# A hybrid attention block on one core: the value loops' banks in two pools, the first key pair's loads inside the value loops, the opening's sums in other banks

## The chip, the core and the metric

The kernel runs on one core of a Trainium2 chip. Five engines with queues of their own work side by side: TensorE (PE, matrix products; the loading of its stationary operand is listed apart as PEld), VectorE (DVE), ScalarE (ACT), GpSimd (POOL) and SyncE (SP), which here only issues transfers. SP and POOL issue the transfers; POOL issues those that add to what is in the destination, and those that depend on its own work. The metric is the device time of one execution in microseconds (us). PE writes into PSUM, eight banks of 512 floats per partition; all other tiles lie in SBUF.

## The reference, cut to what matters

One decoder block on x of 512 tokens by 2048, all in float32: one input projection, two groups of heads, one output projection.

```python
h = _rmsnorm(x, norm_g)
qa, kca, vca, ksa, vsa, kwa, vwa, za, ga, qb, kb, vb, zb = jnp.split(h @ w_in, offsets, axis=-1)
# group A: 8 heads of 128, 2 key/value heads
kc = _compress(_rope(kca), cmp_k_pos, cmp_k_w1, cmp_k_w2)
vc = _compress(vca, cmp_v_pos, cmp_v_w1, cmp_v_w2)
o_cmp, p_cmp = _compressed_attention(qa, kc, vc)
o_sel = _selected_attention(qa, _rope(ksa), vsa, _select_blocks(p_cmp, S))
o_win = _banded_attention(qa, _rope(kwa), vwa, WIN_A)
gates = jax.nn.sigmoid(ga)
y_a = (gates[0] * o_cmp + gates[1] * o_sel + gates[2] * o_win) * jax.nn.silu(za)
# group B: 16 heads of 64, a window of 128 with sinks
y_b = _banded_attention(_rope(qb), _rope(kb), vb, WIN_B, sink=sinks) * jax.nn.silu(zb)
x = x + jnp.concatenate([y_a, y_b], axis=-1) @ w_out
return _rmsnorm(x, final_g)
```

`_compress` takes overlapping blocks of 32 tokens, adds a position table, and sends each block of 32 x 128 numbers through a small two-layer network (w1, silu, w2).

## The kernel before

**Words.** Each float32 operand of a product is split into a high word (rounded, `whi`, `xh`) and a low word (the rest, `wlo`, `xl`), and a product is three matmuls: high by high, high by low, low by high (`mm3`, L107 to L110). So each weight tile is loaded (SP), copied to its high word (ACT, L88 or L517) and subtracted to its low word (DVE, L89 or L518) before PE can use it. There are three buffers for each of the two words, and four for loaded weights, `raw0` to `raw3`.

**Order.** The program is written as one Python function; a scheduler with a model of time orders the instructions of each engine when it is built. Each engine then works through its own queue in that order, and waits at an instruction until its operands and its buffer are free. A tile of a pool is a buffer; a new tile of the same name waits for the last reader of the old one. A pool that takes the room of a closed pool waits for that pool's readers.

**Stages around the change.**

1. Opening (to 60 us). The tokens are loaded, scaled and split; four projections run meanwhile into the six banks of pool `ps0`. Then two sums of squares over the tokens, `psr` and `psc` (L173 to L177), become `rstdb` and `rstd` by ACT (L178, L179) and DVE. `bank(6)` and `bank(7)` are tiles of `psp`, the pool of two banks called `pj` that all projections use.
2. Sliding-window heads (60 to 290). Eight steps of scores, softmax and `attn_b` (L362 on) while PE computes the projections of the next ones (`proj`, L207). `attn_b` ends with a read of its bank `opb` by ACT (L387) and DVE (L388).
3. Value loops (290 to 369, L764 to L780). `tok_chunk` multiplies token chunks into the value accumulators: four units of `wv1` into banks 4 and 5 of pool `ps1`, then eight of `wv0` into banks 0 to 3. Between them `compress_unit` (L646) adds one unit of the compression network to an accumulator `cacc`, each with two loads of `cw`. `build(6)` and `build(7)` make gate weights and sums of token rows (DVE, L408 to L414); the parts stored to `wd` are later loaded over `xh` and `xl` by POOL (L794). `v_evac` (L478) reads the value accumulators.
4. Key pairs `keys(1)` and `keys(0)` (369 to 430), then eight query and gate pairs, `pair(h)` (L634), one per head of group A, between the heads' attention, `attn_a`. Each pair of projections is computed by `seven` (L541): seven products over quarters of the weights instead of eight, called "22", "p", "21", "12", "w", "u" and "q" after what they add up. Products use quarters x1 to x4 and their sums; `tags` says which of `raw0` to `raw3` holds which. For a key pair (`extra`), a fifth buffer `raw5` takes a sum of two quarters, loaded plainly by SP and added to by an accumulating transfer of POOL, and a second such transfer adds into x4 (L565 to L568).
5. Behind the pairs the heads' attention ends and the output projection follows (690 to 843).

In a pair, `turn` applies the rotary table to the query and `q_split` splits it into `qh` and `ql`. For heads 0 to 6 the last add of `turn` and the subtraction for `ql` are on POOL, for head 7 on DVE.

Of the kernel before, what the change touches and what calls it, by code (L numbers as in the profile page):

```python
# [34 lines left out]
def hybrid_block(ctx, tc, xT, xtm, w0, wv0, wv1, wz, wq, wo0, wos, cw1, cw2, cpos, e2, rope, tabs, sinks, gT, fg, out):  # L35
# [134 lines left out]
            o = i * P  # L170
            mm3(acc0[i], hi[:, o:o + P], lo[:, o:o + P], xh[:, k, :], xl[:, k, :], k == 0, k == KT - 1)

    psr = bank(6)  # L173
    pe.matmul(psr, ones, sqa, start=True, stop=True)
    psc = bank(7)
    for t in range(NQ):
        pe.matmul(psc[:, t:t + 1], sqa[:, t * P:(t + 1) * P], ones[:, 0:1], start=True, stop=True)  # L177
    act.activation(rstdb, psr, AF.Sqrt, bias=eps, scale=1.0 / D)  # L178
# [317 lines left out]
            pool.dma_start(Vd[e, :, :, w], other[e].bitcast(F32))  # L496

    ps1s = ExitStack()
    ps1 = ps1s.enter_context(tc.tile_pool(name="ps1", bufs=1, space=PSUM, side="left"))

    def bank(i):
        return ps1.tile([P, S], F32, name=f"bank{i}", tag=f"bank{i}")

    cw2s = pp.tile([P, 2, 2, P], F32, name="cw2s")
    nc.sync.dma_start(cw2s, cw2)
# [22 lines left out]
            ah, al = xf[op, m]  # L528
            mm3(bank, u[0][:, cs], u[1][:, cs], ah, al, new and m == 0, m == 7, not new)

    tags = ["raw0", "raw1", "raw2", "raw3"]

    def load_quarter(src, tag, quarter):
        t = weights(tag)
# [7 lines left out]
    def seven(i, early=(), done=None, hooks=None, extra=None, final=False):  # L542
        src = wq[i]
        early = list(early)
        hooks = hooks or {}
        c1, c2, c4, c3 = tags
        tags[:] = c4, c1, c3, c2

        def load(tag, quarter):
            return early.pop(0) if early else load_quarter(src, tag, quarter)  # L550

        def plus(out, a, b, op=ALU.add):
            return dve.tensor_tensor(out=out, in0=a, in1=b, op=op).ins  # L553

        pa, pb = [psp.tile([P, S], F32, name="pj", tag="pj") for e in range(2)]
        qv = wk.tile([P, S], F32, name="t1", tag="t1", bufs=1)
        zr = wk.tile([P, S], F32, name="zr", tag="xr", bufs=1)
        d, jj = qv[:, H1], zr[:, H0]
        x1 = load(c1, 3)
        u0 = unit(x1)  # L560
        x2 = load(c2, 0)
        u3 = unit(x2)
        x4 = load(c4, 2)
        if extra:
            sm = extra()  # L565
            last["dma"] = nc.sync.dma_start(sm, src[0]).ins
            pool.dma_start(sm, src[2], accum_op=ALU.add)
            pool.dma_start(x4, src[3], accum_op=ALU.add)  # L568
        else:
            sm = x2  # L570
            with ExitStack() as behind:
                if "jj" in last:
                    behind.enter_context(tc.issue_after(last["jj"]))
                plus(x2, x2, x4)
        prod(pb[:, H0], u0, "22", True)
        act.activation(d, pb[:, H0], AF.Copy, scale=-1.0)
        if final:
            act.activation(zr[:, H1], pb[:, H0], AF.Copy)
        run(hooks, "22")
        x3 = load(c3, 1)  # L580
        prod(pa[:, H0], u3, "p", True)
        plus(d, d, pa[:, H0])
        run(hooks, "p")
        if not final:
            u2 = unit(x3)
            prod(pb[:, H0], u2, "21", False)
            act.activation(zr[:, H1], pb[:, H0], AF.Copy)
            plus(jj, d, zr[:, H1])
            run(hooks, "21")
        u4 = unit(sm)  # L590
        if not extra:
            plus(x4, x4, x1)
        plus(sm, sm, x1)
        prod(pa[:, H0], u4, "12", False)
        act.activation(qv[:, H0], pa[:, H0], AF.Copy)
        plus(jj, d if final else jj, qv[:, H0], ALU.subtract)
        run(hooks, "12")
        u1 = unit(x4)
        prod(pa[:, H1], u1, "w", True)
        plus(d, d, pa[:, H1])  # L600
        run(hooks, "w")
        u5 = unit(sm)
        plus(sm, sm, x3)
        prod(pb[:, H1], u5, "u", True)
        last["u"] = recent["mm"]
        plus(d, d, pb[:, H1])
        first = done(qv)
        run(hooks, "u")
        u6 = unit(sm)
        prod(pb[:, H1], u6, "q", False)  # L610
        last["jj"] = plus(jj, jj, pb[:, H1])
        run(hooks, "q")
        if final:
            with tc.issue_after(last["u"]):
                u2 = unit(x3)
                prod(pa[:, H0], u2, "21", True)
            plus(zr[:, H1], zr[:, H1], pa[:, H0])
            plus(jj, jj, zr[:, H1])
        return first, zr
# [13 lines left out]

    def pair(h, hooks=None):  # L634
        def q_done(qv):
            turn(qv, engine=pool if h < 7 else dve)
            return q_split(qv, pool if h < 7 else dve)

        qq, zr = seven(2 + h, done=q_done, hooks=hooks, final=h == 7)
        last["jj"] = dve.tensor_tensor(out=zr, in0=zr, in1=rstdb, op=ALU.mult).ins  # L640
        st = wk.tile([P, S], F32, name="st", tag="st")
        act.activation(st, zr, AF.Tanh, scale=0.5)
        dve.scalar_tensor_tensor(out=st, in0=st, scalar=1.0, in1=zr, op0=ALU.add, op1=ALU.mult)
        return qq, st
# [38 lines left out]
        return sl  # L683

    def compressed_keys(acc):
        sl = compress_hidden(acc, bank(4))
        kcp = bank(5)
        for i in range(2):
            pe.matmul(kcp[:, 0:64], cw2s[:, 0, i, :], sl[:, i, :], start=i == 0, stop=i == 1)
        kct = pp.tile([P, 64], F32, name="kct")  # L690
        act.activation(kct, kcp[:, 0:64], AF.Copy, scale=0.5)
        k1 = pp.tile([P, 2, CMP], F32R, name="k1w")
        for g, (h, l) in enumerate(((KH[:, 0:CMP], KL[:, 0:CMP]), (k1[:, 0], k1[:, 1]))):
            src = kct[:, g * 32:g * 32 + 32]
            act.activation(h, src, AF.Copy)
            dve.tensor_tensor(out=l, in0=src, in1=h.bitcast(F32), op=ALU.subtract)
        for e in range(2):
            pool.dma_start(Kd[e, :, 0:CMP], k1[:, e].bitcast(F32))

    def compressed_values(acc):  # L700
        sl = compress_hidden(acc, bank(4))
        for g in range(2):
            sr = wk.tile([P, 2, 4, 32], F32, name="sr", tag="pcr", bufs=1)
            for i in range(2):
                dve.tensor_copy(sr[:, i], sl[:, i, g * 32:g * 32 + 32].unsqueeze(1).to_broadcast([P, 4, 32]))
            vcp = bank(5 - g)
            for i in range(2):
                pe.matmul(vcp[:, 0:P], sr[:, i].rearrange("p a b -> p (a b)"), cw2s[:, 1, i, :], start=i == 0,
                          stop=i == 1)
# [17 lines left out]
                pool.dma_start(Kd[e, :, CMP:].rearrange("p (t w c) -> p w t c", w=2, c=P)[:, w],  # L727
                                  views[e].bitcast(F32))

    def fifth():  # L730
        return pp.tile([P, 1056], F32, name="raw5", tag="kvt0")[:, 0:1024]

    def keys(g, hooks, early=()):
        def one(v):
            turn(v)
            key_words(v, g, 0)

        zr = seven(1 - g, early, done=one, hooks=hooks, extra=fifth)[1]

        def other():  # L740
            turn(zr)
            key_words(zr, g, 1)

        return other
# [15 lines left out]
        turned(kc[g], kvts[0][:, g, :, 0:32])  # L760
    for g in range(2):
        values(proj(wz[18 + g]), g)
    cacc = [psp.tile([P, S], F32, name="pj", tag="pj") for e in range(2)]
    xr = rows(6)  # L764
    for u in range(4):
        tok_chunk(wv1, 4, 256, vacc[1], u, True)
# [6 lines left out]
            build(7, xr)  # L773
    for u in range(8):
        tok_chunk(wv0, 2, 280, vacc[0], u, False)
        compress_unit(1, u, cacc[1])
        if u == 0:
            v_evac(1, vacc[1])
        if u == 1:
            compressed_keys(compress_sum(cacc[0]))  # L780

    def gate_evac():
        for t in range(NQ):
# [3 lines left out]
        gc = gates[:, 0, :].rearrange("p (h b) -> p h b", b=3)[:, :, 0]  # L787
        dve.tensor_scalar(gc, gc, rowvalid, None, op0=ALU.mult)

    early = [load_quarter(wq[0], c, quarter) for c, quarter in zip(tags, (3, 0, 2, 1))]  # L790
    with tc.issue_after(last["lo"]):
        for ms in (slice(0, 4), slice(4, 8)):
            for e in range(2):
# [568 lines left out]
```

## Time and profile before

| | us |
|---|---|
| median of three runs | 844.12 |
| the three runs | 840.61, 844.12, 848.92 |
| the profiled execution | 845.09 |
| its span | 843.3 |
| PE busy | 807.7 (96%) |
| DVE busy | 688.8 (82%) |
| ACT busy | 500.4 (59%) |
| POOL busy | 97.4 (12%) |

The profile is of one execution, whose own time is 845.09 us; the span of 843.3 runs from its first to its last instruction. All positions are us from the span's start. A row of a timeline has the start, the duration, the engine, the line, the operation, and the tile written and the tiles read; in brackets is how long the engine had been idle before it and what ended that. "x2" means two such instructions in a row. A row of waits has who waited, for what, how long in total, how often, and the longest. Lines such as L108 are lines of the kernel before; a helper's line stands for all its callers, so the tile names tell the caller.

### The profile page before, as it was taken

To read this page: it belongs to the slowest core of one execution; us is meant where nothing else is said; L and a number is where in the kernel's file an instruction comes from. 1 tells how busy PE (TensorE), PEld (TensorE's weight loads), DVE (VectorE), ACT (ScalarE), POOL (GpSimd) and SP (SyncE) were. 2 spreads that over 40 slices of the span, in tenths; PEclk is the share of its full clock that TensorE was granted. 3 is DMA by queue.
4 is the path that set the end of the run, shared out by engine and by line. 5 is a ranking of instruction groups with operands and counts; after the bars stand their busy time and mean duration, and the time that the engine had idled before them with its cause. 6 is when DMAs were issued, how large, how long until landed. Compare 5 with 4: busy or idle time off the path is not lost.

```text
span 843.3 us, 15353 instructions
## 1 busy us (share of the span) xinstructions
PE 807.7 (96%) x5738; PEld 751.2 (89%) x5738; DVE 688.8 (82%) x1404; ACT 500.4 (59%) x1092; POOL 97.4 (12%) x93
## 2 busy tenths in 40 slices
PE   9989999999999899989899999999989899999996
PEld 7777888888888789989799999999989799999996
DVE  6768988988897567748889998998998978777995
ACT  6635655645555346654447678777677767544545
POOL 3514000000010001332101110110010000010000
PEclk9999999999999999999999999999999999999998
DMA  8552143144343338967333223234245126796845
GB/s 283 164 175 93 58 150 114 62 125 150 125 136 115 126 86 267 293 206 200 125 101 83 65 67 113 62 104 164 89 146 167 51 79 249 223 229 203 231 114 200
DMA packets 45450, 122.12 MB, mean 145 GB/s; under 512 B 5408, under 2 KB 7488, under 8 KB 45376
## 3 DMA queue, kind: packets, MB, share of 16 engines
q1 hardware_dynamic: 41504, 108.00, 39.2%
q0 software_dynamic: 3584, 12.62, 7.2%
q8 instruction: 45, 0.74, 0.4%
q10 hardware_dynamic: 288, 0.52, 0.2%
q14 instruction: 29, 0.24, 0.1%
HBM read 108.77 MB, written 12.35 MB: 144 GB/s over the span
## 4 chain that ended last, share of the span: by engine, by line
PE 72%; DVE 12%; DMA 6%; ACT 5%; issue 4%; SPq 0%; POOL 0%; DVEq 0%; ACTq 0%; POOLq 0%
PE pj L108 14%; PE pj L109 14%; PE pj L110 14%; PE oa L109 4%; PE oa L110 4%; PE oa L108 4%; PE sp L832 3%; DVE wlo L518 2%; PE bank L109 2%; DMA raw<-wq 2%; PE bank L108 2%; PE bank L110 2%; PE tp L371 1%; DVE raw L553 1%; DVE wlo L89 1%
## 5 line engine op out<-in xcount | busy, mean ns | idle before, releaser
L108 PE MATMUL pj<-xh,whi 128*128 128x256 f32 (+1 forms) x608 | 204.2, 336 | 8.6 <-ACT rstdb L178 2.7
L110 PE MATMUL pj<-xh,wlo 128*128 128x256 f32 (+1 forms) x608 | 203.0, 334 | 0.9 <-DVE wlo L518 0.8
L109 PE MATMUL pj<-xl,whi 128*128 128x256 f32 (+1 forms) x608 | 203.1, 334 | 0.0
L108 PEld LDWEIGHTS pj<-xh,whi 128*128 128x128 f32 x608 | 115.0, 189 | 20.8 <-ACT rstdb L178 2.8
L110 PEld LDWEIGHTS pj<-xh,wlo 128*128 128x128 f32 x608 | 114.8, 189 | 12.0 <-DVE wlo L518 1.5
L109 PEld LDWEIGHTS pj<-xl,whi 128*128 128x128 f32 x608 | 114.9, 189 | 11.1 <-issue 0.7
L89 DVE TENSOR_TENSOR wlo<-raw,whi 128x1024 fp32r<-128x1024 f32 (+2 forms) x72 | 80.9, 1127 | 31.1 <-ACT whi L88 26.5
L517 ACT ACTIVATE whi<-raw 128x1024 fp32r<-128x1024 f32 x70 | 73.3, 1056 | 49.2 <-PE pj L109 20.9
L88 ACT ACTIVATE whi<-raw 128x1024 fp32r<-128x1024 f32 (+2 forms) x71 | 65.0, 920 | 61.1 <-PE pj L109 48.1
L518 DVE TENSOR_TENSOR wlo<-raw,whi 128x1024 fp32r<-128x1024 f32 x70 | 87.0, 1252 | 12.1 <-ACT whi L517 11.8
L109 PE MATMUL oa<-wlo,yh 128*128 128x256 f32 x200 | 55.9, 280 | 0.2 <-DVE wlo L1185 0.2
L110 PE MATMUL oa<-whi,yl 128*128 128x256 f32 x200 | 55.8, 279 | 0.0
L108 PE MATMUL oa<-whi,yh 128*128 128x256 f32 x200 | 55.6, 279 | 0.0
L108 PE MATMUL pj<-pu,whi 128*128 128x256 f32 x160 | 45.6, 285 | 4.0 <-ACT a L672 1.8
L110 PE MATMUL pj<-pu,wlo 128*128 128x256 f32 x160 | 45.0, 281 | 0.0
L109 PE MATMUL pj<-pu,whi 128*128 128x256 f32 x160 | 44.7, 280 | 0.0
L272 DVE TENSOR_TENSOR pl<-tp,ph 128x512 fp32r<-128x512 f32 x56 | 37.6, 683 | 6.2 <-ACT ph L271 5.9
L350 ACT ACTIVATE ttb<-ttb,sums 128x256 f32<-128x256 f32 (+1 forms) x64 | 30.0, 471 | 16.7 <-DVE sums L343 16.5
L271 ACT ACTIVATE ph<-tp 128x512 fp32r<-128x512 f32 x56 | 31.7, 590 | 12.4 <-PE tp L867 11.1
L553 DVE TENSOR_TENSOR raw<-raw 128x1024 f32<-128x1024 f32 x32 | 38.9, 1216 | 0.1
L109 PEld LDWEIGHTS oa<-wlo,yh 128*128 128x128 f32 x200 | 37.8, 189 | 0.4 <-DVE wlo L1185 0.4
L110 PEld LDWEIGHTS oa<-whi,yl 128*128 128x128 f32 x200 | 37.8, 189 | 0.0
(372 smaller groups left out, 2340.3 us busy)
## 6 DMA issues: line engine op xcount, KB each, us to landing
raw<-wq SPq DMA_DIRECT2D x42, 512.0 KB, 4.1
raw<-wz SPq DMA_DIRECT2D x36, 512.0 KB, 3.9
cw<-cw SPq DMA_DIRECT2D x32, 256.0 KB, 4.2
raw<-wos SPq DMA_DIRECT2D x12, 512.0 KB, 6.5
rw<-wos SPq DMA_DIRECT2D x10, 512.0 KB, 5.4
xr<-xT SPq DMA_DIRECT2D x16, 256.0 KB, 4.4
rows<-xT SPq DMA_DIRECT2D x8, 512.0 KB, 5.2
raw<-wo SPq DMA_DIRECT2D x8, 512.0 KB, 3.8
```

What stands on the lines that cost most here:

```text
L88: last["hi"] = act.activation(hi[:, :width], rw[:, :width], AF.Copy).ins
L89: last["lo"] = dve.tensor_tensor(out=lo[:, :width], in0=rw[:, :width], in1=hi[:, :width].bitcast(F32), op=ALU.subtract).ins
L108: pe.matmul(ps, ah, bh, start=first, stop=False, skip_group_check=go_on)
L109: pe.matmul(ps, ah, bl, start=False, stop=False, skip_group_check=go_on)
L110: recent["mm"] = pe.matmul(ps, al, bh, start=False, stop=last, skip_group_check=go_on).ins
L271: act.activation(ph, tp, AF.Copy)
L272: dve.tensor_tensor(out=pl, in0=tp, in1=ph.bitcast(F32), op=ALU.subtract)
L350: act.activation(tv, tv, AF.Exp, bias=mn[:, e, v:v + 1], scale=-1.0, accum_out=dn[:, e, v:v + 1])
L517: act.activation(hi, src, AF.Copy)
L518: last["lo"] = dve.tensor_tensor(out=lo, in0=src, in1=hi.bitcast(F32), op=ALU.subtract).ins
L553: return dve.tensor_tensor(out=out, in0=a, in1=b, op=op).ins
L832: pe.matmul(sp[:, a:b], qq[:, qs], kk[:, ko:ko + b - a], start=pi == 0, stop=pi == 2)
```

## The change

**Opening.** The two sums of squares go to banks 0 and 1 of `ps0` instead of the two `pj` buffers.

**Value loops.** Pool `ps1` of six banks becomes two pools, banks 0 to 3 on the left and banks 4 and 5 on the right. The second compression accumulator is bank 4, taken when the first value loop's accumulators have been read out, and no longer a `pj` buffer; the small banks of the compressed keys and values are renumbered to fit. The accumulator of the compressed keys is copied one unit earlier.

**Key pairs.** `tags` starts with another order, so that x1 of the first pair lies in `raw3`. Inside the second value loop, x1 is loaded at unit 3, and the first pair's sum at unit 4; the other three quarters are loaded behind the loop. The second pair's sum gets a buffer of its own (`kvt1`). For a key pair `tags` is turned once more, so that the next pair finds other buffers.

**Query pairs.** Head 6 has its last rotary add and its `ql` on DVE, as head 7.

```diff
-    psr = bank(6)
+    psr = bank(0)
...
-    psc = bank(7)
+    psc = bank(1)
...
-    ps1 = ps1s.enter_context(tc.tile_pool(name="ps1", bufs=1, space=PSUM, side="left"))
+    ps1 = [ps1s.enter_context(tc.tile_pool(name=f"ps1{side[0]}", bufs=1, space=PSUM, side=side)) for side in ("left", "right")]
 
     def bank(i):
-        return ps1.tile([P, S], F32, name=f"bank{i}", tag=f"bank{i}")
+        return ps1[i // 4].tile([P, S], F32, name=f"bank{i}", tag=f"bank{i}")
...
-    tags = ["raw0", "raw1", "raw2", "raw3"]
+    tags = ["raw3", "raw0", "raw1", "raw2"]
...
         x4 = load(c4, 2)
         if extra:
             sm = extra()
-            last["dma"] = nc.sync.dma_start(sm, src[0]).ins
-            pool.dma_start(sm, src[2], accum_op=ALU.add)
             pool.dma_start(x4, src[3], accum_op=ALU.add)
+            tags[:] = c2, c1, c4, c3
...
-            turn(qv, engine=pool if h < 7 else dve)
-            return q_split(qv, pool if h < 7 else dve)
+            turn(qv, engine=pool if h < 6 else dve)
+            return q_split(qv, pool if h < 6 else dve)
...
-    def fifth():
-        return pp.tile([P, 1056], F32, name="raw5", tag="kvt0")[:, 0:1024]
+    def fifth(n):
+        return pp.tile([P, 1056], F32, name="raw5", tag=f"kvt{n}")[:, 0:1024]
+
+    def sums(t, src, first, other):
+        last["dma"] = nc.sync.dma_start(t, src[first]).ins
+        pool.dma_start(t, src[other], accum_op=ALU.add)
+
+    def fifth_sum(g):
+        if ready:
+            return ready.pop()
+        t = fifth(1)
+        sums(t, wq[1 - g], 0, 2)
+        return t
...
-        zr = seven(1 - g, early, done=one, hooks=hooks, extra=fifth)[1]
+        zr = seven(1 - g, early, done=one, hooks=hooks, extra=lambda: fifth_sum(g))[1]
...
-    cacc = [psp.tile([P, S], F32, name="pj", tag="pj") for e in range(2)]
+    cacc = [psp.tile([P, S], F32, name="pj", tag="pj"), None]
+    early, ready = [], []
...
         tok_chunk(wv0, 2, 280, vacc[0], u, False)
-        compress_unit(1, u, cacc[1])
         if u == 0:
             v_evac(1, vacc[1])
+            csum = compress_sum(cacc[0])
+            cacc[1] = bank(4)
+        compress_unit(1, u, cacc[1])
         if u == 1:
-            compressed_keys(compress_sum(cacc[0]))
+            compressed_keys(csum)
+        if u == 3:
+            early.append(load_quarter(wq[0], tags[0], 3))
+        if u == 4:
+            ready.append(fifth(0))
+            sums(*ready, wq[0], 0, 2)
...
-    early = [load_quarter(wq[0], c, quarter) for c, quarter in zip(tags, (3, 0, 2, 1))]
+    early += [load_quarter(wq[0], c, quarter) for c, quarter in zip(tags[1:], (0, 2, 1))]
```

**Where instructions moved.** On PE at the start of the value loops (banks 4 and 5 are the first value accumulators, `pj_2913` the last projection ahead of the compression), before:

```order
L110 MATMUL bank4_2837<-whi_2980,xl_105 128x256
L108 MATMUL bank5_2838<-whi_2980,xh_104 128x256
L108 MATMUL pj_2913<-xh_104,whi_2915 128x512
L109 MATMUL pj_2913<-xl_105,whi_2915 128x512
L110 MATMUL pj_2913<-xh_104,wlo_2916 128x512
```

and in the changed kernel, where that projection is `pj_2916`:

```order
L108 MATMUL bank5_2841<-whi_2982,xh_104 128x256
L109 MATMUL bank5_2841<-wlo_2983,xh_104 128x256
L110 MATMUL bank5_2841<-whi_2982,xl_105 128x256
L108 MATMUL pj_2916<-xh_104,whi_2918 128x512
L109 MATMUL pj_2916<-xl_105,whi_2918 128x512
```

Before, the projection came after 31 of the first value unit's 48 matmuls, and the other 17 followed it; now it comes after all 48.

On DVE in the same place (`cw` and `wlo_3066` belong to the compression, `rows` to `pu` to `build(6)`, `kvt1<-pj` is the read-out of that projection, `wlo_3102` the second value unit's low word), before:

```order
L747 TENSOR_TENSOR kvt1_2830<-pj_2913,rstdb_68 128x16x32
L518 TENSOR_TENSOR wlo_3066<-cw_3067,whi_3065 128x512
L518 TENSOR_TENSOR wlo_3066<-cw_3071,whi_3065 128x512
L408 TENSOR_TENSOR rows_2977<-rows_2977 128x256
L409 SCALAR_TENSOR_TENSOR rows_2977<-rows_2977,gt_70 128x256
L656 COPY F_3258<-posw_2826 128x4x2 x2
L410 SCALAR_TENSOR_TENSOR rows_2977<-rows_2977,gt_70 128x256
L89 TENSOR_TENSOR wlo_3102<-raw_3100,whi_3101 128x1024
L414 SCALAR_TENSOR_TENSOR qw1_600<-rows_2977,gt_70,qw0_599 128x256
```

and in the changed kernel, where that low word is `wlo_3104`:

```order
L518 TENSOR_TENSOR wlo_3068<-cw_3073,whi_3067 128x512
L408 TENSOR_TENSOR rows_2979<-rows_2979 128x256
L409 SCALAR_TENSOR_TENSOR rows_2979<-rows_2979,gt_70 128x256
L410 SCALAR_TENSOR_TENSOR rows_2979<-rows_2979,gt_70 128x256
L414 SCALAR_TENSOR_TENSOR qw1_600<-rows_2979,gt_70,qw0_599 128x256
L414 SCALAR_TENSOR_TENSOR pu3_594<-rows_2979,pu1_592 128x256
L411 TENSOR_TENSOR rows_2979<-rows_2979 128x256
L414 SCALAR_TENSOR_TENSOR pu7_598<-rows_2979,pu5_596 128x256
L414 SCALAR_TENSOR_TENSOR wf_3085<-rows_2979,wf_3085 128x256
L757 TENSOR_TENSOR kvt1_2833<-pj_2916,rstdb_68 128x16x32
L655 COPY F_3260<-posw_2829 128x4x2
L89 TENSOR_TENSOR wlo_3104<-raw_3102,whi_3103 128x1024
```

Before, the second value unit's low word came after three steps of `build(6)`; now all eight and the projection's read-out (L757 in the changed kernel) stand ahead of it.

On SP at the end of the value loops (`cw` are the last compression weights, `raw` the first pair's quarters), before:

```order
L662 DMA cw_3847<-cw1 128x512
L535 DMA raw_3918<-wq 128x1024
L662 DMA cw_3898<-cw1 128x512
L662 DMA cw_3902<-cw1 128x512
L535 DMA raw_3914<-wq 128x1024
L535 DMA raw_3916<-wq 128x1024
```

and in the changed kernel, with `raw5_4237` the second pair's sum and `raw_3924` the first pair's x4:

```order
L661 DMA cw_3855<-cw1 128x512
L535 DMA raw_3926<-wq 128x1024
L733 DMA raw5_4237<-wq 128x1024
L661 DMA cw_3906<-cw1 128x512
L661 DMA cw_3910<-cw1 128x512
L535 DMA raw_3922<-wq 128x1024
L535 DMA raw_3924<-wq 128x1024
```

The second pair's sum has come in ahead of the last two `cw`, and x4 is now the last of the quarters. On POOL in the same place, before, with `raw_3918` the first pair's x4:

```order
L568 DMA raw_3918<-wq 128x1024
L794 DMA xh_104<-wd_75 128x4x256
L794 DMA xl_105<-wd_75 128x4x256
L494 TENSOR_TENSOR VL_2810<-vt_3978,VH_2809 128x128
L494 TENSOR_TENSOR v1_3977<-vt_3978,v1_3976 128x128
```

and in the changed kernel:

```order
L734 DMA raw5_4237<-wq 128x1024
L812 DMA xh_104<-wd_75 128x4x256
L812 DMA xl_105<-wd_75 128x4x256
L566 DMA raw_3924<-wq 128x1024
L494 TENSOR_TENSOR VL_2810<-vt_3981,VH_2809 128x128
```

Before, the accumulation into x4 stood ahead of the second pair of `wd` loads; now the accumulation into the second pair's sum has that place, and the one into x4 follows those loads.

More of the change, by code (lines that the diff above doesn't have):

```diff
@@ L685, in compressed_keys @@
     def compressed_keys(acc):
-        sl = compress_hidden(acc, bank(4))
+        sl = compress_hidden(acc, bank(5))
         kcp = bank(5)
@@ L700, in compressed_values @@
     def compressed_values(acc):
-        sl = compress_hidden(acc, bank(4))
+        sl = compress_hidden(acc, bank(5))
         for g in range(2):
@@ L705, in compressed_values @@
                 dve.tensor_copy(sr[:, i], sl[:, i, g * 32:g * 32 + 32].unsqueeze(1).to_broadcast([P, 4, 32]))
-            vcp = bank(5 - g)
+            vcp = bank(4 + g)
             for i in range(2):
```

## The prediction

> **What bounds the kernel now.** I read the page first, then the table by stage, then what TensorE (PE) waits for in each stage that leaves it idle, and last the rows of the engines that end those waits.
>
> The page: the span, the busy share of each engine, and the chain that ended last.
>
> ```profile
> span 843.3 us, 15353 instructions
> PE 807.7 (96%) x5738; PEld 751.2 (89%) x5738; DVE 688.8 (82%) x1404; ACT 500.4 (59%) x1092; POOL 97.4 (12%) x93
> PE 72%; DVE 12%; DMA 6%; ACT 5%; issue 4%; SPq 0%; POOL 0%; DVEq 0%; ACTq 0%; POOLq 0%
> ```
>
> PE is busy 807.7 of 843.3 us, so the change does nothing for the products themselves; all it can win is among the 35.6 us in which PE stands still, and in the time it runs at a lower clock. The table by stage says where those lie (busy time of PE, weight loads, VectorE (DVE), ScalarE (ACT), GpSimd (POOL); then granted clock, DMA share, GB/s).
>
> ```profile
> 50.00:60.00 10.00, 7.28 (x35) 5.77 (x34) 7.03 (x6) 4.24 (x5) 0.00 (x0) 1.00 0.63 208
> 60.00:280.00 220.00, 218.74 (x1124) 183.99 (x1123) 188.30 (x466) 119.91 (x283) 19.44 (x12) 1.00 0.35 113
> 280.00:295.00 15.00, 11.95 (x67) 10.28 (x66) 7.68 (x11) 5.80 (x11) 0.00 (x0) 0.93 0.35 105
> 312.00:360.00 48.00, 47.19 (x383) 46.30 (x382) 36.12 (x96) 31.08 (x82) 9.24 (x15) 1.00 0.86 265
> 360.00:375.00 15.00, 12.71 (x100) 12.10 (x98) 6.65 (x13) 7.34 (x15) 2.89 (x5) 1.00 0.74 223
> 400.00:430.00 30.00, 25.99 (x221) 25.24 (x220) 26.92 (x34) 12.32 (x17) 3.10 (x4) 1.00 0.30 92
> 600.00:686.00 86.00, 78.75 (x613) 76.02 (x612) 79.77 (x191) 62.27 (x159) 2.57 (x2) 0.96 0.40 126
> ```
>
> Long stretches (60 to 280, 312 to 360) are bound by PE, so a gain made ahead of them is carried through. In 312 to 360 the DMA engines are the second limit (0.86). In 400 to 430 and 600 to 686 VectorE is nearly as full as PE. The losses sit at five seams, and the change touches all five.
>
> **1. The opening's sums in other banks.** The two sums of squares took the two projection buffers; the next projection waits until ScalarE has read them.
>
> ```profile
> 54.71 0.69 ACT L178 ACTIVATE rstdb<-pj,small 128x512 f32<-128x512 f32 x1
> 55.45 0.50 PE L108 MATMUL pj<-xh,whi 128*128 128x512 f32 x1 [2.72 <-ACT rstdb L178]
> 75.60 1.22 DVE L89 TENSOR_TENSOR wlo<-raw,whi 128x1024 fp32r<-128x1024 f32 x1
> 77.98 0.69 DVE L113 TENSOR_TENSOR t<-pj,cosA 128x512 f32<-128x512 f32 x1 [1.16 <-PE tp L438]
> 80.13 0.50 PE L108 MATMUL pj<-xh,whi 128*128 128x512 f32 x1 [1.26 <-DVE t L115]
> ```
>
> With banks 0 and 1 that wait is gone, and PE runs 2.72 us ahead. But its next stop is VectorE: a projection buffer comes free only after the three rotary steps that begin at 77.98, and these stand behind the step of 75.60, which ends at 76.82 whatever PE does. They can move up by 77.98 - 76.82 = 1.16, no more. So 1.1 of the 2.72 are kept (bounds 0, if VectorE's earlier steps slip, and 2.7). Nothing else is issued or moved here.
>
> **2. The start of the value loops.** The loops' six banks were one pool that could open only when the last sliding-window head's output had been read out; the change gives the value accumulators two banks of their own on the other side.
>
> ```profile
> PE bank L108 <- DVE ob L388: 3.0, 1, 3.0
> 288.44 1.23 DVE L89 TENSOR_TENSOR wlo<-raw,whi 128x1024 fp32r<-128x1024 f32 x1 [4.19 <-PE pj L110]
> 290.92 0.68 DVE L388 TENSOR_TENSOR ob<-opb,ob 64x512 f32<-64x512 f32 x1 [0.66 <-ACT ob L387]
> 292.90:296.30 3.40, 3.40 (x19) 3.40 (x18) 3.37 (x5) 0.90 (x4) 0.00 (x0) 0.50 0.77 204
> 627.40:630.80 3.40, 3.40 (x17) 3.40 (x18) 3.40 (x5) 2.17 (x8) 0.00 (x0) 0.50 0.73 258
> 303.11 1.29 DVE L518 TENSOR_TENSOR wlo<-cw,whi 128x512 fp32r<-128x512 f32 x2 [3.17 <-ACT whi L517]
> 308.11 1.07 DVE L747 TENSOR_TENSOR kvt<-pj,rstdb 128x512 f32<-128x512 f32 x1 [3.71 <-PE pj L110]
> 312.83 0.47 DVE L414 SCALAR_TENSOR_TENSOR qw<-rows,gt,qw 128x256 fp32r<-128x256 f32 x1
> 312.97 0.39 PE L109 MATMUL bank<-wlo,xh 128*128 128x256 f32 x1 [0.44 <-DVE wlo L89]
> ```
>
> PE waited 3.05 us for the read-out, and then ran 3.4 us at a clock of 0.50, which costs 3.4 x 0.5 = 1.7. The next wait in the old order, 0.44 at 312.97, belongs to the same knot. New waits take part of it back. PE starts at 288.7 on words whose low half is ready at 288.44 + 1.23 = 289.67, and two matmuls cover 0.23: 0.75 of waiting. Then the orders of PE and VectorE have turned as well. PE does all 48 products of the first value unit ahead of the last projection (31 before), so that projection starts 3.05 + 1.7 - 0.75 = 4.0 sooner less 17 matmuls of 0.12 (47.19 us for 383 in the row of 312), 1.9 sooner in all, and ends at 308.1 - 1.9 = 306.2. Behind it come 16 compression products (2.0), so PE wants the next unit's low half at 308.2. VectorE has, ahead of that half, the step of 303.11 (two halves, 1.9 sooner, to 302.5), eight steps of the gate weights (0.47 as at 312.83, 3.7 in sum, to 306.2), the step of 308.11 (1.07, to 307.3) and the half itself (1.2): 308.5, 0.3 to 0.4 of waiting. Net 3.05 + 1.7 + 0.44 - 0.75 - 0.4 = 4.0 (bounds 0 and 5.2).
>
> Here stands a rule of the Trainium skill against a term. "TensorE: Matmul & The Clock Gate", Part 1, has the clock halved only after an idle window of about 3.4 us. By it no wait here is long enough, the 1.7 is not the wait's doing, and the sum below would be 7.3 and not 9.0. This trace has 0.50 right behind a wait of 3.05 us, and again at 627.4 behind one of 1.9; I go by the trace.
>
> **3. Into the first key pair.** These are the PE waits of 366 to 380, then what VectorE, POOL and the DMA engines do there.
>
> ```profile
> PE pj L108 <- ACT a L672: 1.8, 1, 1.8
> PE pj L110 <- DVE wlo L518: 0.8, 1, 0.8
> PE pj L108 <- ACT whi L517: 0.7, 1, 0.7
> 366.03 1.29 DVE L518 TENSOR_TENSOR wlo<-cw,whi 128x512 fp32r<-128x512 f32 x2 [2.96 <-ACT whi L517]
> 368.43 0.28 PE L668 MATMUL pj<-wlo,F 128*128 128x256 f32 x1
> raw<-wq POOLq DMA_DIRECT2D x1, 512.0 KB, 9.2
> 372.49 0.75 POOL L794 DMA_DIRECT2D xl<-wd  x1 [5.12 <-issue]
> 393.42 6.08 DMA raw<-wq
> ```
>
> The quarter that the first product needs comes now early in the loop, and the accumulator's bank is no longer a projection buffer: all three waits go, 0.71 + 0.76 + 1.76 = 3.2. Two things are paid. On SP's queue the second pair's plain sum (512 KB) is issued ahead of the last two compression weights. At 308 GB/s (265 / 0.86, the row of 312) that is 1.7 us; the weights' low half was ready at 366.03 + 1.29 = 367.3 and first used at 368.4, so 0.6 is seen. On POOL's queue the accumulation into raw_3924, issued third in that group before, is issued last, behind the wd loads: at about 373.2. Accumulations took 6.08 us (the row at 393.42) and 9.2 (the row of the one issued at 360.59, beside loads). Taking the middle, it lands at 380.8, is split by 383.1 (1.07 + 1.22), and PE, now 3.2 ahead, wants it at 381.9: 1.2 of waiting. Net 3.2 - 0.6 - 1.2 = 1.4 gained. Bounds: 3.2 gained, with neither seen; 3.0 lost, with 1.7, 2.8 (landing at 382.4) and a clock drop of 1.7.
>
> **4. The second key pair.** Its sum was issued late, and ScalarE stood behind it.
>
> ```profile
> 399.61 1.06 ACT L517 ACTIVATE whi<-raw 128x1024 fp32r<-128x1024 f32 x1 [3.41 <-DMA raw<-wq]
> 402.56 0.38 ACT L576 ACTIVATE t<-pj 128x256 f32<-128x256 f32 x1 [0.43 <-DVE k L724]
> 403.00 0.38 PE L108 MATMUL pj<-xh,whi 128*128 128x256 f32 x1 [2.13 <-ACT t L576]
> 409.35 0.39 PE L108 MATMUL pj<-xh,whi 128*128 128x256 f32 x1 [0.47 <-ACT t L595]
> ```
>
> The sum now lands in the loop, so 2.13 + 0.47 can go. VectorE is busy 26.92 of 30 there and has the same work left, so its 3.1 of room is not all usable: I take 1.5 (bounds 0 and 2.6).
>
> **5. Head 6's rotary add and split from POOL to VectorE.**
>
> ```profile
> 623.61 1.28 POOL L243 TENSOR_TENSOR ql<-t,qh 128x512 fp32r<-128x512 f32 x1 [3.66 <-ACT qh L242]
> L643 DVE SCALAR_TENSOR_TENSOR st<-st,zr x8: 675/682/1357, 447.2 to 664.7; 128x512 f32<-128x512 f32 x8
> 649.17 0.69 DVE L627 TENSOR_TENSOR t<-t,t 128x512 f32<-128x512 f32 x1
> PE sp L832 <- DVE sums L838: 4.9, 4, 1.9
> ```
>
> VectorE gets two steps of 0.69 (head 7's, in the row of 649.17). It gets 0.67 back: L643 took 1.357 beside POOL's step and 0.682 otherwise. Net +0.7 on an engine with 86 - 79.77 = 6.2 us of room in 600 to 686. In exchange the score sums come ahead of a word split, and the wait of 1.9 at 625.4 shrinks by about 1.4, perhaps with its clock drop. VectorE being nearly full, I keep 1.0 (bounds 3.7 gained, its gaps closed; 0.7 lost).
>
> **Sum.** 1.1 + 4.0 + 1.4 + 1.5 + 1.0 = 9.0 off 845.09, the profiled execution's own time (span 843.3 and 1.8 around it): 836.1. That execution lies 0.97 above the median of 844.12, within the runs of 840.61 to 848.92.
>
> **Rivals.** B, all seams clear: the accumulation lands in time and the weights are not late (1.8 more), the second pair gets all (1.1 more), the end closes VectorE's gaps (2.7 more): 830.5. For it: the waits are there, named, and each named cause goes. Against it: VectorE's load.
>
> C, the DMA engines eat the loop's gain. In 312 to 360 they move 265 GB/s at 0.86, so 308 when full as above, and 0.14 x 48 x 308 = 2.07 MB are free. The sum adds 1.05 MB, and a loop 4.0 us earlier wants 1.23 MB sooner: 2.28. The loop then ends where it ended: 840.1. For it: that arithmetic has no slack. Against it: the first loads may be made in the stretch of 295 to 312, and what is late at the loop's end costs only where no buffer covers it.
>
> D, slower: the same, and worse behind it. With the engines full into the pair, the accumulation at the end of POOL's queue takes 9.2 us or more, VectorE's split of it blocks all behind it, and the clock drops: 4.0 lost, 4.4 in the transition (from 1.4 gained to 3.0 lost), 1.5 in the second pair: 846.0. It decides when that accumulation lands after 379.6 on the old clock, and in earnest from 382. For it: 9.2 was measured. "DMA: Bandwidth & Descriptors", Issuing engines are not separate DMA queues, in the Trainium skill, says that transfers started by different engines share the same 16 and interleave, so SP's loads are no cover for POOL's; the 9.2 beside loads against 6.08 agrees.
>
> **How the numbers follow.** A change below about 1%, 8.4 us, can't be told from none in this kernel, so faster is under 835.7 and slower over 852.6. The forecast A has 0.44 (its own range 833 to 840, 0.16 of it under 835.7); B 0.26, all faster; C 0.17, all within 1%; D 0.13, about half of it beyond 852.6 (0.07) if more transfers fall behind. Faster 0.16 + 0.26 = 0.42, same 0.28 + 0.17 + 0.06 = 0.51, slower 0.07. The range runs from 829.5, just below B, to 848, just above D.
>
> **What would show it.** Step 1: no wait for rstdb near 53, and one of about 2 for the rotary steps near 77. Step 2: no wait for ob L388, clock 1.0 near 290, the waits of 0.75 and 0.4 on wlo. Step 3: the three waits gone, and the landing of raw_3924's accumulation against its use. Step 4: no ScalarE wait for the sum. Step 5: L643 at 0.68 in head 6. The forecast is wrong if the value loops end less than 3 us earlier relative to their start's shift, or if the DMA share in the loop reaches 1.0 with new waits on raw.

## The result and the profile after

| | kernel before | changed kernel |
|---|---|---|
| median of 20 runs, us | 848.03 (840.61 to 855.83) | 840.59 (838.85 to 843.23) |
| ratio, 95% interval | | 0.9919 (0.9900 to 0.9938) |
| profiled execution, its span | 845.09, 843.3 | 840.15, 838.4 |

The change makes the kernel 0.8% faster: by the ratio 0.0081 x 848 = 6.9 us, where 9.0 were forecast. The time of 840.59 lies in the forecast's range of 829.5 to 848, 4.5 above its number. The two profiled executions are 4.9 us apart and not 6.9; the experiment on the opening gives a likely reason.

The page of the changed kernel, and its table by stage (columns as before).

```profile
span 838.4 us, 15343 instructions
PE 806.3 (96%) x5738; PEld 749.4 (89%) x5738; DVE 689.7 (82%) x1406; ACT 500.0 (60%) x1092; POOL 93.1 (11%) x91
PE 67%; DVE 14%; DMA 8%; issue 5%; ACT 3%; POOL 1%; SPq 0%; ACTq 0%; POOLq 0%; DVEq 0%
```

```profile
50.00:60.00 10.00, 10.00 (x48) 8.08 (x47) 5.95 (x5) 5.31 (x6) 0.00 (x0) 1.00 0.60 206
280.00:295.00 15.00, 14.22 (x95) 12.55 (x94) 7.82 (x12) 5.81 (x11) 0.00 (x0) 1.00 0.34 107
360.00:375.00 15.00, 14.80 (x125) 14.60 (x124) 9.76 (x13) 8.88 (x21) 7.07 (x12) 1.00 0.84 218
375.00:400.00 25.00, 20.08 (x148) 19.51 (x147) 19.06 (x31) 9.83 (x16) 3.02 (x4) 0.86 0.54 144
400.00:430.00 30.00, 26.33 (x216) 25.42 (x216) 25.42 (x32) 11.89 (x16) 2.27 (x3) 1.00 0.30 90
600.00:686.00 86.00, 80.48 (x645) 78.04 (x644) 79.91 (x195) 63.77 (x159) 0.00 (x0) 0.98 0.41 132
```

Three seams are closed: PE is busy 10.00 of 10 in 50 to 60 (7.28 before), 14.22 of 15 in 280 to 295 at full clock (11.95 at 0.93), 14.80 of 15 in 360 to 375 (12.71). A new hole stands in 375 to 400: 20.08 of 25, at a clock of 0.86.

Both kernels issue 5738 matmuls, so the start of the n-th one in each execution can be set side by side. The table, worked out from the traces, shows by how many us PE is ahead of the profiled execution of the kernel before. The kernels behind the first column are those of the next section. At most rows the work done up to there is the same in all kernels; at the 2200th matmul up to 2 products differ, and at the 4500th up to 20.

```
matmul  before at  changed  acc_first  acc_sr  no_keys  pools_alone  opening_alone  head6_alone
  400      90.8      0.2       0.4      -1.0     0.4       -1.9          2.6            0.1
 1400     282.5      0.2       0.4      -1.0     0.4       -1.9          2.6            0.1
 1900     356.9      4.1       4.7       3.4     4.9        1.4          2.7           -1.4
 2000     371.4      6.0       6.6       5.3     6.8        3.3          4.5           -0.5
 2200     397.6      2.1       6.4       7.4     8.0        5.6          4.9           -0.5
 2500     438.5      0.9       5.4       8.7     2.2       -0.8          1.4           -0.3
 4000     620.7      1.1       5.6       6.6     2.2       -1.0          1.4           -0.3
 4500     693.1      4.7       7.9       9.5     5.0       -1.8          1.1            3.0
 5700     831.3      4.8       4.7       9.5     4.8       -2.4          0.0            3.0
```

The changed kernel wins 4 us in the value loops. It is 8.2 ahead at the 2046th matmul (379 before), when the old waits of the first key pair are behind it, loses all but 0.9 of this by 438, and wins 3.6 in head 6 and behind. Up to the 1400th matmul the columns mostly show how early the opening's loads came in that execution.

Where most of it went can be read from a few rows. POOL, ScalarE, VectorE and PE of the changed kernel, at the first key pair, and the clock behind it:

```profile
368.49 0.75 POOL L812 DMA_DIRECT2D xl<-wd  x1 [5.22 <-PE pj L110]
369.23 0.96 POOL L566 DMA_DIRECT2D raw<-wq  x1
377.06 1.06 ACT L517 ACTIVATE whi<-raw 128x1024 fp32r<-128x1024 f32 x1 [6.28 <-DMA raw<-wq]
378.15 1.22 DVE L518 TENSOR_TENSOR wlo<-raw,whi 128x1024 fp32r<-128x1024 f32 x1 [3.94 <-ACT whi L517]
381.23 1.22 PE L707 MATMUL bank<-cw2s,sr 128*128 128x128 f32 x4 [3.97 <-DVE sr L704]
380.20:387.00 6.80, 5.77 (x27) 5.77 (x28) 5.87 (x13) 2.98 (x5) 0.93 (x1) 0.50 0.82 195
```

The last wd load waits 5.22 us on POOL for PE; the accumulation into x4 is behind it. ScalarE idles 6.28 us for its landing, and behind x4's high word on ScalarE and low word on VectorE stand the steps that lead to `sr`, which PE needs first. PE stands still 3.97 us; then the clock is 0.50 for 6.8 us, of which PE is busy 5.77, so the drop costs 2.9 more.

### The profile page after: what moved, and what is told of

Same layout as the page of the kernel before. It is cut to its first block, busy times and chain, and to the rows that moved or that the text cites. A ratio compares the mean times of both kernels' runs of the same rounds, so it can differ in the third digit from the quotient of the medians.

```text
span 838.4 us, 15343 instructions
## 1 busy us (share of the span) xinstructions
PE 806.3 (96%) x5738; PEld 749.4 (89%) x5738; DVE 689.7 (82%) x1406; ACT 500.0 (60%) x1092; POOL 93.1 (11%) x91
## 3 DMA queue, kind: packets, MB, share of 16 engines
q1 hardware_dynamic: 41504, 108.00, 39.5%
## 4 chain that ended last, share of the span: by engine, by line
PE 67%; DVE 14%; DMA 8%; issue 5%; ACT 3%; POOL 1%; SPq 0%; ACTq 0%; POOLq 0%; DVEq 0%
PE pj L108 13%; PE pj L109 13%; PE pj L110 13%; PE oa L109 3%; PE oa L110 3%; PE oa L108 3%; PE sp L850 3%; DMA xr<-xT 3%; DVE wlo L518 2%; DMA rw<-wos 2%; DMA raw<-wq 2%; PE bank L109 2%; PE bank L110 1%; PE tp L371 1%; PE bank L108 1%
## 5 line engine op out<-in xcount | busy, mean ns | idle before, releaser
L518 DVE TENSOR_TENSOR wlo<-raw,whi 128x1024 fp32r<-128x1024 f32 x70 | 88.7, 1276 | 14.3 <-ACT whi L517 14.0
L866 ACT ACTIVATE tt<-tt,sums 128x128 f32<-128x128 f32 (+3 forms) x64 | 35.3, 553 | 4.8 <-DVE sums L856 4.5
L108 PEld LDWEIGHTS oa<-whi,yh 128*128 128x128 f32 x200 | 37.8, 189 | 0.0
```

Source lines behind the costliest of these rows:

```text
L108: pe.matmul(ps, ah, bh, start=first, stop=False, skip_group_check=go_on)
L518: last["lo"] = dve.tensor_tensor(out=lo, in0=src, in1=hi.bitcast(F32), op=ALU.subtract).ins
L866: act.activation(tv, tv, AF.Exp, bias=mn[:, i, 1 + w:2 + w], scale=-1.0, accum_out=dn[:, i, 1 + w:2 + w])
```

## The experiments

Theory A: that accumulation, late because it is behind the wd loads, alone makes the hole. Theory B: VectorE is the bound there (one low word took 3.34 us), and the transfers don't matter.

**The accumulation ahead of the last wd load (acc_first).**

```diff
-            pool.dma_start(x4, src[3], accum_op=ALU.add)
+            last["acc"] = pool.dma_start(x4, src[3], accum_op=ALU.add).ins
+            run(hooks, "acc")
...
-        for ms in (slice(0, 4), slice(4, 8)):
-            for e in range(2):
-                pool.dma_start(even[e][:, ms], wd[e, :, ms])
+        for e, ms in ((0, slice(0, 4)), (1, slice(0, 4)), (0, slice(4, 8))):
+            pool.dma_start(even[e][:, ms], wd[e, :, ms])
+
+    def last_wd():
+        with tc.issue_after(last["acc"]):
+            pool.dma_start(even[1][:, 4:8], wd[1, :, 4:8])
...
-    other = keys(1, {"22": [
+    other = keys(1, {"acc": [last_wd], "22": [
```

> The changed kernel with one order turned: the accumulation into the first pair's x4 is issued ahead of the last wd load on POOL's queue, not behind it. Theory A (the late accumulation alone makes the wait of 3.97 us at 377.3 and the 6.8 us at a clock of 0.50 behind it): it is issued near 366.4 instead of 369.2, lands near 374, the wait falls under 1 and the clock stays at 1.0; 5 to 7 us less than the changed kernel, ratio to the kernel before about 0.985. Theory B (VectorE is the bound there: its low word took 3.34 us beside POOL's subtractions, and the steps behind it follow in order): the accumulation lands earlier but PE still waits 2 to 4 us there; under 1.5 us gained, ratio 0.990 to 0.992.

Measured: 838.86, ratio 0.9862 (0.9820 to 0.9903). POOL and PE of that run:

```profile
367.17 0.86 POOL L566 DMA_DIRECT2D raw<-wq  x1 [4.48 <-DVE gates L807]
PE bank L708 <- DVE sr L705: 2.0, 1, 2.0
```

The accumulation is issued 2.1 us sooner (its queue now waits for VectorE and not for PE), the wait halves and the clock stays at 1.0 there: at 438 PE is 5.4 ahead and not 0.9, and 0.6 of this it had at 357. B falls; in the changed kernel VectorE had also been idle 3.94 us just ahead of x4's low word, as the row above shows. A was too simple: 2.0 us of wait remain, so some 4 us came and not the 5 to 7. In this execution the output projection ran slower and took about 3 us of it back (last section). The times alone would not settle it: the median is 1.7 us under the changed kernel's, and the two intervals of the ratio overlap.

**The compressed values ahead of x4's words (acc_sr).** In that run `sr` still stood behind x4's words, through its activation `th`. The edit is on top of acc_first.

```diff
+        last["th"] = act.activation(th, hp[:, 0:P], AF.Tanh, scale=0.5).ins
...
+            last.setdefault("sr", copied)
...
-        u1 = unit(x4)
+        with ExitStack() as behind:
+            if extra:
+                behind.enter_context(tc.issue_after(last["sr"]))
+                behind.enter_context(tc.issue_after(last["th"]))
+            u1 = unit(x4)
```

> The accumulation first on POOL's queue, as before, and the compressed values' activation and copies ahead of x4's words on ScalarE and VectorE. In the run with the accumulation first, PE still waited 1.97 us for the copy sr, whose activation stood behind x4's high word. Theory A' (the rest of the wait is that order): the wait goes to under 0.5, 1.5 to 2 us less than with the accumulation alone, 5 to 7 less than the changed kernel in the lead at 430, ratio to before about 0.984. Theory B' (PE then waits for x4's words themselves, or the time comes back in the second pair): the lead at 430 grows by less than 0.7 over the run with the accumulation alone.

Measured: 835.0 (832.99 to 835.87), ratio 0.9833 (0.9810 to 0.9857); the changed kernel, measured beside it (changed_again):

> The changed kernel once more, as the measure for the other runs of this call. Both theories: ratio to the kernel before 0.990 to 0.994, the wait of about 4 us at 377 with a clock of 0.50 behind it again. If the trace shows a different stretch in which the matmuls of the output projection follow each other by 118 ns in place of 113 ns, that pace belongs to the execution and not to the kernel.

It had 840.91, ratio 0.9912 (0.9891 to 0.9932), with the wait at 3.83 us and 0.50 behind it, for one window of 3.4 us this time. So the two turned orders are worth about 6 us. PE's waits of acc_sr in the whole of 360 to 400:

```profile
PE pj L108 <- DVE t L553: 0.6, 1, 0.6
PE pj L108 <- ACT t L595: 0.5, 1, 0.5
PE pj L108 <- DVE zr L553: 0.4, 1, 0.4
```

The wait for `sr` is gone, so A' holds; the lead at 438 grows by 3.3 over acc_first, more than the 1.5 to 2 expected, because a wait of 1.35 us in the second pair goes as well. Some 2 us of that lead are lost again by 621. This version is faster than both kernels: 14 us below before.

**The read-out ahead in the second pair (acc_sr_copy).** This edit is on top of acc_sr.

```diff
+        last["d"] = act.activation(d, pb[:, H0], AF.Copy, scale=-1.0).ins
...
+            with ExitStack() as behind:
+                if second:
+                    behind.enter_context(tc.issue_after(last["d"]))
+                u2 = unit(x3)
```

> As the last one, and in the second key pair the read-out of the first product (ScalarE, the copy with scale -1) goes ahead of the words of x3. In the changed kernel that product was done at 393.3 and its copy came at 400.84, behind a high word that waited for a free buffer; PE waited 1.35 us for it. If the order is the cause: that wait goes, 1 to 1.5 us more lead at 430 than in the kernel without it. If VectorE is the bound in the second pair: the wait reappears at another of its products, under 0.5 us.

Measured: 834.63, ratio 0.9837 (0.9814 to 0.9860), level with acc_sr, and no more lead at 438 (8.5 against 8.7, with an opening 2 us earlier). In acc_sr PE had already stopped waiting for that read-out: none of the three waits above is for it. Here a later read-out of the second pair costs 0.6, and the wait for the same read-out in the first query pair, near 412, goes from 0.9 to 0.6. The edit brings nothing.

**The changed kernel without the key pair part (no_keys), and the two pools alone (pools_alone).** No_keys takes back `tags`, `fifth`, the sums and the early loads; pools_alone is the kernel before with this part of the change, and with the renumbered small banks and the earlier copy of the accumulator that go with it:

```diff
-    ps1 = ps1s.enter_context(tc.tile_pool(name="ps1", bufs=1, space=PSUM, side="left"))
+    ps1 = [ps1s.enter_context(tc.tile_pool(name=f"ps1{side[0]}", bufs=1, space=PSUM, side=side)) for side in ("left", "right")]
...
-        return ps1.tile([P, S], F32, name=f"bank{i}", tag=f"bank{i}")
+        return ps1[i // 4].tile([P, S], F32, name=f"bank{i}", tag=f"bank{i}")
...
-    cacc = [psp.tile([P, S], F32, name="pj", tag="pj") for e in range(2)]
+    cacc = [psp.tile([P, S], F32, name="pj", tag="pj"), None]
...
+            cacc[1] = bank(4)
```

> The changed kernel without its key pair part (tags, early loads and sums as before), with the opening, the two pools and head 6. Theory A: the key pair part cost more than it saved (PE's lead over the kernel before fell from 4.1 us at the loop's end to 0.9 at 438), so this one keeps a lead of 4 through the key pairs and is 2 to 4 us faster than the changed kernel, ratio about 0.988. Theory B: the key pair part still saved its three waits, this one is level with the changed kernel or up to 2 us slower, ratio 0.991 to 0.995.

> The kernel before with the two pools alone (and the accumulator and the compressed banks that go with them). If the first part of the gain is the wait of 3.05 us and its clock drop: the lead over the kernel before is 4 to 5 us from 300 to 360, and 7 to 8 by 395, of which the second pair takes 4 back for its late sum; ratio about 0.996. If the pools' gain needs the early loads: the lead is gone by 375, ratio 0.999 to 1.0.

Measured: no_keys 841.25, ratio 0.9910 (0.9886 to 0.9935), level with the changed kernel; pools_alone 847.39, ratio 0.9971 (0.9951 to 0.9990). PE's wait in the second pair, of no_keys and of pools_alone, and ScalarE of the latter:

```profile
PE pj L108 <- ACT t L576: 5.2, 2, 4.3
```

```profile
PE pj L108 <- ACT t L576: 5.7, 1, 5.7
398.48 1.06 ACT L517 ACTIVATE whi<-raw 128x1024 fp32r<-128x1024 f32 x1 [7.85 <-DMA raw<-wq]
```

Without the key part PE comes through the first pair 8.0 ahead (5.6 in pools_alone from -1.9, so 7.5 won), and stops in the second one: its sum lands too late. So the pools also clear the old waits at the first pair (0.7, 0.8, 1.8), without the early loads. The key part cures the second pair's late sum and makes the first pair's x4 late instead; neither theory had that.

**The key pair part alone (keys_alone).** The kernel before with the hunks on `tags`, `seven`, `fifth`, `keys` and the loads in the loop.

```diff
+        if u == 3:
+            early.append(load_quarter(wq[0], tags[0], 3))
+        if u == 4:
+            ready.append(fifth(0))
+            sums(*ready, wq[0], 0, 2)
```

> The kernel before with the key pair part alone. Theory A: the accumulation is late here as well, PE waits 3 to 4 us in the first pair with a clock drop behind it, and the kernel is 1 to 4 us slower than before, ratio 1.001 to 1.005. Theory B: three waits go (3.2 us) and a shorter one comes, 0 to 2 us faster, ratio 0.998 to 1.0.

Measured: 849.4, ratio 1.0020 (0.9990 to 1.0051): no gain. The new wait at the first pair is there without the lead that the pools bring:

```profile
PE bank L707 <- DVE sr L704: 2.3, 1, 2.3
```

**Head 6 back on POOL (head6_pool), and on VectorE alone (head6_alone).** The first is the changed kernel, the second the kernel before, with

```diff
-            turn(qv, engine=pool if h < 7 else dve)
-            return q_split(qv, pool if h < 7 else dve)
+            turn(qv, engine=pool if h < 6 else dve)
+            return q_split(qv, pool if h < 6 else dve)
```

turned back in the first and made in the second.

> The changed kernel with head 6's rotary add and ql back on POOL. If the 3.7 us of lead that came after 620 belong to that move: 3 to 4 us slower than the changed kernel, ratio about 0.996, the wait on the score sums near 620 back at 1.5 to 2 and a window of 0.50 behind it. If they belong to the order of the end only: under 1 us, ratio 0.992.

> The kernel before with head 6's rotary add and ql on VectorE, nothing else. If the lead of 3.7 us near 625 is that part's own: 3 to 4 us less, ratio 0.9955 to 0.9965, the wait on the score sums near 625 at about 0.6 and not 1.9, and VectorE's step on st near 624 at 0.68 and not 1.36. If it needed the lead of the other parts (another phase of the clock's windows): 1 to 2 us less.

Measured: head6_pool 843.67, ratio 0.9942 (0.9921 to 0.9963), 3.1 us above the changed kernel's median and 2.0 by the ratios; head6_alone 845.67, ratio 0.9957 (0.9932 to 0.9983). PE's waits from 600 to 686 in head6_pool, then in head6_alone with the step on `st`:

```profile
PE sp L850 <- DVE sums L856: 4.9, 4, 1.9
```

```profile
PE sp L832 <- ACT qh L242: 1.9, 1, 1.9
PE sp L832 <- DVE sums L838: 0.9, 2, 0.6
L643 DVE SCALAR_TENSOR_TENSOR st<-st,zr x8: 674/680/691, 447.7 to 665.7; 128x512 f32<-128x512 f32 x8
```

The part wins its 3 to 4 us by itself. The score sums' wait falls from 4.9 to 0.9, and no step on `st` takes 1.36 any more. Another wait, 1.9 for a `qh`, stands in its place.

**The opening alone (opening_alone).** The kernel before with

```diff
-    psr = bank(6)
+    psr = bank(0)
...
-    psc = bank(7)
+    psc = bank(1)
```

> The kernel before with the opening's sums in banks 0 and 1, nothing else. If VectorE's chain is what holds the rest, as forecast: the wait for rstdb near 53 is gone, PE's idle time from 50 to 82 falls from 3.7 to 4.0 us to 2.5 to 2.9, and in those executions in which the wait was followed by a clock of 0.50 (two of the three without this part that were traced) another 1.7 goes: 1 to 2.5 us less, ratio 0.997 to 0.999. If PE's whole lead of 2.7 is kept: ratio 0.996 or less, and no longer wait for the rotary steps near 79.

Measured: 845.59, ratio 0.9967 (0.9945 to 0.9990), 2.8 us. PE's waits from 40 to 84:

```profile
PE pj L108 <- DVE t L115: 1.5, 1, 1.5
PE tp L438 <- issue: 0.9, 1, 0.9
```

In sum 2.45 instead of the 2.72 + 1.26 = 3.98 of before: 1.5. The rest fits the clock. The wait of 2.72 had none behind it in the execution that I worked from; three other executions without this part (keys_alone, pools_alone, head6_alone) show one:

```profile
55.60:59.00 3.40, 3.40 (x10) 2.63 (x9) 3.40 (x3) 0.00 (x0) 0.00 (x0) 0.50 0.67 228
```

```profile
56.90:60.30 3.40, 3.40 (x10) 2.62 (x9) 3.40 (x5) 0.00 (x0) 0.00 (x0) 0.50 0.80 270
```

```profile
54.80:58.20 3.40, 3.40 (x10) 2.64 (x9) 3.40 (x4) 0.00 (x0) 0.00 (x0) 0.50 0.71 249
```

None of the eight traced executions with the part does. At a clock of 0.50 these 3.4 us cost 1.7. This is a likely part of why the profiled execution of before is 3 us under its median, and why the pair of profiles shows less than the ratio; it is not shown, as only one execution of that kernel was traced. In the pair itself the opening's loads came about a microsecond later in the changed kernel, and hid the gain (0.2 in the table).

## Why the prediction was right, point by point

The time fell in the range, the sign was right, and the sum (9.0) came near the 6.9 measured. But of its five terms only the one of the value loops came out as forecast. The others missed in both directions and partly cancelled, so that the total came near is in part luck.

1. **Opening, 1.1 forecast.** The mechanism was right. VectorE's step of 76.65 now runs straight into the rotary steps, the idle 1.16 ahead of them is gone, and PE waits for them:

```profile
76.65 1.23 DVE L89 TENSOR_TENSOR wlo<-raw,whi 128x1024 fp32r<-128x1024 f32 x1
77.80 0.68 DVE L113 TENSOR_TENSOR t<-pj,cosA 128x512 f32<-128x512 f32 x1
79.94 0.50 PE L108 MATMUL pj<-xh,whi 128*128 128x512 f32 x1 [1.54 <-DVE t L115]
```

In the pair itself PE's waits from 40 to 84 fall by 1.05 us, as forecast: 1.54 and a new 1.39 stand for 2.72 and 1.26. As a time the size was off (2.8 in opening_alone): I priced one execution, whose 2.72 us of waiting lay across two windows of the clock and cost no drop.

2. **Value loops, 4.0 forecast.** Right: the lead goes from 0.2 to 4.1. The wait for `ob` is gone, the clock is 1.00, and the new wait on the low word is 0.78 where 0.75 was forecast; the second one, 0.4, did not show. Rival C, the DMA engines eating this, did not happen: their share from 312 to 360 is 0.84 and PE is busy 47.70 of 48.

```profile
312.00:360.00 48.00, 47.70 (x385) 46.98 (x384) 31.90 (x83) 29.44 (x74) 9.98 (x16) 1.00 0.84 267
289.57 0.39 PE L109 MATMUL bank<-wlo,xh 128*128 128x256 f32 x1 [0.78 <-DVE wlo L89]
```

Of the 23 windows of the clock (last section) in which PE was idle for over 2.0 us, in all traces, 21 were followed by 0.50 and the other two were at 0.50 already. The rule of the Trainium skill, "TensorE: Matmul & The Clock Gate", Part 1, by which it takes an idle window of about 3.4 us, and which would have struck the 1.7, did not hold here.

3. **First key pair, 1.4 gained forecast, about 3 lost measured** (a lead of 4.1 at 357, 8.2 at the 2046th matmul, 1.0 at the 2202nd). This is the step that failed. All three old waits went, as said, and the 0.6 for late weights did not show. The accumulation came when it was forecast: it was issued at 369.2 and landed at 376.95, which is 373.3 and 381.0 on the old clock, 4.1 later; 373.2 and 380.8 were forecast. But I let PE want x4 at 381.9 on the old clock, for its own product, and put only x4's words ahead of it. Behind those words stood, on two engines, the steps to `sr`, and PE wanted `sr` first, at 377.3. The wait was 3.97 and not 1.2, and the half clock behind it, for which the sum had nothing, cost 2.9. This is rival D's place, with its split on VectorE and its clock drop; the accumulation took 7.7 us and not 9.2, and D's other half, the lost loop gain, did not come. The wait and the drop went past the 2.8 and 1.7 of the lower bound; the loss as a whole reached its 3.0. Acc_first and acc_sr show the cause: the two orders undone give back 6 us.

4. **Second key pair, 1.5 gained forecast, nothing measured** (1.0 at the 2202nd matmul, 0.9 at 438). The table's row of 2200 shows 2.1, because it stands just ahead of the stop with which the first pair ends, PE's wait for VectorE's last step of that pair:

```profile
396.84 0.36 PE L108 MATMUL pj<-pu,whi 128*128 128x256 f32 x1 [0.86 <-DVE zr L553]
```

From there to the 2490th matmul both kernels need the same time, 39.5 us now and 39.4 before, though PE's waits fall from 5.2 to 4.6: it now stops six times and not five, and each stop delays the next starts by some 0.25 us beyond its idle time. ScalarE no longer waits for the sum. But its next word starts only when the product ahead of it ends, at 399.9; the profile names no cause for that, and a buffer that PE must free is my guess. The read-out is again behind that word:

```profile
399.88 1.06 ACT L517 ACTIVATE whi<-raw 128x1024 fp32r<-128x1024 f32 x1 [2.40 <-issue]
400.84 0.37 ACT L575 ACTIVATE t<-pj 128x256 f32<-128x256 f32 x1
401.26 0.39 PE L108 MATMUL pj<-xh,whi 128*128 128x256 f32 x1 [1.35 <-ACT t L575]
```

I had named what goes and not what is late next. That the early sum is needed all the same is shown by no_keys and pools_alone, where a PE that comes early waits 4.3 and 5.7 us for it.

5. **Head 6, 1.0 forecast, 3.6 measured.** The mechanism was right, with the size of rival B (3.7): the wait of 1.9 became 0.6, and the drop behind it went (another came at 649.8, behind the wait of 1.9 for `qh`). Keeping only 1.0 because VectorE is nearly full was the mistake: VectorE's busy time from 600 to 686 is the same (79.77 and 79.91), and its order set the wait. The waits did not all go: a new one of 2.8 for a low word stands at 671.9, without a drop behind it.

```profile
PE sp L850 <- ACT qh L242: 1.9, 1, 1.9
PE sp L850 <- DVE sums L856: 0.6, 1, 0.6
PE pj L109 <- DVE wlo L89: 2.8, 1, 2.8
```

The parts alone measure 2.8 (opening), 2.5 (pools), -1.7 (keys) and 3.6 (head 6), 7.2 together and about what the change gives; the intervals of each are some 2 us wide to either side.

## What to carry to other kernels

When a wait at the head of a stage is taken away, the stage behind it is entered earlier, and the next thing that has not moved with it becomes the wait: here a transfer issued by an engine whose queue holds something that waits for PE. So price a moved transfer by what stands ahead of it on its queue with the new arrival time, and list what stands behind its consumer on each engine, not only the consumer. And price a wait from several executions: the opening's wait of 2.1 to 2.7 us had a clock drop worth 1.7 behind it in three executions and none in a fourth, as it lay in the clock's windows.

## What the runs showed of the hardware that was not expected

**The clock's windows.** In all twelve traces the changes of the granted clock lie on a grid of 3.413 us that is fixed within an execution. By PE's idle time in each window of that grid that ran at 1.00: with 1.0 to 1.6 us, one window in 58 was followed by 0.50; with 1.6 to 2.0, 6 of 16; with over 2.0, all 21. So a wait of 1.9 us costs 1.9 or 3.6, by chance. A window at 0.50 was followed by another in all 6 cases in which PE was idle in it for over 1.0 us, and in one of the other 29. The wait for `sr` shows it: in the changed kernel's first trace it reached 1.08 us into the window at 0.50, which was followed by a second one; in changed_again it ended ahead of that window, and there was only one.

**Two paces of the same matmuls.** In the output projection PE is never idle and the clock is 1.00, yet the same products follow each other by 113 ns in one execution and 118 in another. From 730 to 810, the changed kernel and acc_first:

```profile
730.00:810.00 80.00, 80.00 (x709) 80.00 (x708) 66.45 (x75) 39.32 (x51) 8.67 (x10) 1.00 0.80 208
```

```profile
730.00:810.00 80.00, 80.00 (x682) 80.00 (x681) 65.46 (x75) 38.28 (x50) 8.67 (x10) 1.00 0.76 205
```

That is 27 matmuls, 3 us, in 80 us. In all traces the pace is near 120 ns from 690 up to about 710 to 720 and then 113; acc_first went back to 118 from 730 to 810, others at most near the end. The cause stays open; a median over runs is needed where 3 us matter.

**VectorE beside POOL.** A low word that takes 1.2 us took 3.34 while POOL ran its eight subtractions in the changed kernel. It is not the same each time: beside these subtractions a low word took 3.3 to 3.8 us in six of the twelve traces, and 1.5 to 1.6 in the other six. The step on `st` took 1.36 in place of 0.68 beside POOL's `ql` before.

```profile
370.54 3.34 DVE L518 TENSOR_TENSOR wlo<-raw,whi 128x1024 fp32r<-128x1024 f32 x1 [1.19 <-ACT whi L517]
```
